# Attention's mask as a TensorE product under the scores, maxima and exponentials read from PSUM

## The chip, the cores and the metric

One core of a Trainium2 chip runs one layer of a decoder trunk. The metric is device time in microseconds of one execution, the median of several runs. Engines: TensorE (PE; PEld is its weight load), VectorE (DVE), ScalarE (ACT), GpSimd (POOL) and SyncE (SP), which issues most DMAs.

## The reference

1024 tokens of width 1024, one layer, float32. Cut to what matters here:

```python
h = x @ w_in                                  # -> q (8 heads x 64), k, v (2 x 64), conv_a, conv_gate
scores = einsum('bnqkgd,bnskd->bnkgqs', qb, kb) * 64 ** -0.5   # blocks of 128, keys of two blocks
scores = where(valid, scores, -1e30)          # window of 128: causal and not too old
m = maximum(max(scores, -1), sink)
e = exp(scores - m)
probs = e / (sum(e, -1) + exp(sink - m))
out = probs @ v
```

Beside attention a convolution group (gated, 31 taps, layer norm, swish) is computed from `conv_a` and `conv_gate`. Both go through `w_out`, a residual and a layer norm. Then comes PEER (product keys, the top 16 of 8 heads, experts from tables `peer_u` and `peer_v` of 16384 rows), a gated embedding and a last layer norm.

## The kernel before

**Tiling.** The 8 blocks of 128 tokens are split in group A (blocks 0 to 2) and group B (3 to 7). The string `ORDER` weaves generators, one for each stage and group: `q0`, `q1` (q, k and v), `c0`, `c1` (gate products of the convolution), `t0`, `t1` (its taps, 31 VectorE instructions for each of 4 channel blocks, line 351), `a0`, `a1` (attention), `l0`, `l1`, `w0`, `w1` (`w_out`), `n0`, `n1` (layer norm), `y` (PEER queries of group A), `h` and `u`. What is traced in that order is then laid out for every engine but GpSimd by a planner, which simulates the program with its own costs and lets an engine take what is ready, the earlier in the traced order first. Each engine then runs its list in order.

**Attention** (`s_att`). For each block, q and k are turned by TensorE (lines 373, 377) and copied by ScalarE (374, 379). Then `scores(g)` runs for each of two groups of four heads; one such call is called a pass below, 16 in all. It takes two PSUM banks of the pool tag `pt` (two buffers in all). The four heads lie two to a bank: heads 0 and 2 in the first, 1 and 3 in the second. The products (line 390) write `nb` x 128 columns a head: 256, or 128 in block 0, which has no block before it. Line 394 (VectorE, once a bank) scales by 0.125, adds the mask and writes `sc`, a page of SBUF. Line 400 takes the maxima, lines 401 to 403 combine them with the sink and negate, line 406 (ScalarE) makes the exponentials and their sums, 408 and 409 the reciprocals, 411 scales. `values(g)` follows up to two passes later: it turns `sc` through `pt` (line 422), copies it (423) and multiplies by v (426).

**What else uses `pt`:** the transposes of the layer norm (line 261) and those of the `u` blocks (654). The tags `ph` (four banks) and `pv` (two) hold the other products.

**Weights** (`w_split`, line 264): a DMA on SP, then ScalarE's rounded half (156) and VectorE's rest (152). The products of three halves are lines 160 to 162.

**PEER queries** (`s_query`): for each of 8 heads two products, then the scores against `keysT`, loaded by SP (line 545) into one of three buffers, and read at line 556.

Of the kernel before, what the change touches and what calls it, by code (L numbers as in the profile page):

```python
# [8 lines left out]
F32 = mybir.dt.float32  # L9
F32R = mybir.dt.float32r  # L10
BF = mybir.dt.bfloat16
I32 = mybir.dt.int32
U32 = mybir.dt.uint32
AF = mybir.ActivationFunctionType
OP = mybir.AluOpType
AX = mybir.AxisListType
# [3 lines left out]
P = 128  # L20
# [78 lines left out]
def layer(tc, io):  # L99
    nc = tc.nc  # L100
# [12 lines left out]
    def pool(name, side):  # L113
        p = tc.tile_pool(name=name, bufs=1, side=side, reuse_waits="tile")
        opened.append(p)
        return p, p.__enter__()
# [17 lines left out]
    def pt():  # L134
        return PP.tile([P, 512], F32, name="pt")
# [11 lines left out]
    def pv():  # L147
        return PP.tile([P, 512], F32, name="pv")
# [15 lines left out]
    ident = C.tile([P, P], F32, name="ident")  # L164
# [20 lines left out]
    def page(shape, dt, name):  # L185
        return PG.tile(shape, dt, name=name, tag="page", bufs=PAGES)
# [7 lines left out]
    def bcast(src, name, pool_=None):  # L194
# [4 lines left out]
    W, W_ = pool("front", "right")  # L199
# [7 lines left out]
    mask = W_.tile([P, 2 * P], BF, name="mask")  # L207
# [2 lines left out]
                            pattern=[[1, P]], channel_multiplier=-1)  # L210
    nc.gpsimd.affine_select(out=mask[:, P:], in_=mask[:, P:], compare_op=OP.is_ge, fill=-1e30, base=0,
                            pattern=[[-1, P]], channel_multiplier=1)
    ones = W_.tile([P, P], F32, name="ones")
    nc.gpsimd.memset(ones, 1.0 / 512.0)
    halo = W_.tile([P, 4, HALO], F32, name="halo")
    nc.gpsimd.memset(halo, 0.0)
    kT, vt = {}, {}
# [137 lines left out]
    def s_att(gi):  # L355

        later = []
        for j, i in enumerate(groups[gi]):
            qkv = work[i]
            rv = qkv[:, :768].rearrange("p (h d) -> p h d", d=64)  # L360
            cos = trig[:, 0, i, None, :].to_broadcast([P, 12, 8])
            sin = trig[:, 1, i, None, :].to_broadcast([P, 12, 8])
            tm = W_.tile([P, 4, 12, 8], F32, name="rot")
            nc.gpsimd.tensor_tensor(tm[:, 0], rv[:, :, 0:8], cos, op=OP.mult)
            nc.gpsimd.tensor_tensor(tm[:, 1], rv[:, :, 8:16], sin, op=OP.mult)
            nc.gpsimd.tensor_tensor(tm[:, 2], rv[:, :, 8:16], cos, op=OP.mult)
            nc.gpsimd.tensor_tensor(tm[:, 3], rv[:, :, 0:8], sin, op=OP.mult)
            nc.gpsimd.tensor_tensor(rv[:, :, 0:8], tm[:, 0], tm[:, 1], op=OP.subtract)
            nc.gpsimd.tensor_tensor(rv[:, :, 8:16], tm[:, 2], tm[:, 3], op=OP.add)
            qT = W_.tile([P, 4, P], F32, name="qT")  # L370
            ps = pt()
            for k in range(4):
                nc.tensor.transpose(ps[:, k * P:(k + 1) * P], qkv[:, k * P:(k + 1) * P], ident)
            nc.scalar.copy(qT, ps.rearrange("p (k t) -> p k t", k=4))
            ps = pt()
            for k in range(2):
                nc.tensor.transpose(ps[:, k * P:(k + 1) * P], qkv[:, 512 + k * P:512 + (k + 1) * P], ident)
            kT[i] = W_.tile([P, 2, P], F32, name="kT", bufs=3)
            nc.scalar.copy(kT[i], ps[:, :2 * P].rearrange("p (g t) -> p g t", g=2))
            nb = 2 if i else 1  # L380
            S = nb * P
            outs = {}

            def scores(g):
                sc = page([P, 4, 2 * P], F32, "sc")
                pse = [pt(), pt()]
                for pr in range(2):
                    for e in range(2):
                        for b in range(nb):
                            nc.tensor.matmul(pse[e][:, pr * S + b * P:pr * S + (b + 1) * P],  # L390
                                             qT[e * 64:e * 64 + 64, 2 * g + pr, :],
                                             kT[i + 1 - nb + b][e * 64:e * 64 + 64, g, :], start=True, stop=True)
                for e in range(2):
                    nc.vector.scalar_tensor_tensor(
                        sc[:, e::2, :S], pse[e][:, :2 * S].rearrange("p (r s) -> p r s", r=2), 0.125,
                        mask[:, None, 2 * P - S:].to_broadcast([P, 2, S]), op0=OP.mult, op1=OP.add)
                st = W_.tile([P, 3, 4], F32, name="st", bufs=4)
                nm, den, sk = st[:, 0], st[:, 1], st[:, 2]
                sg = sink[:, 4 * g:4 * g + 4]
                nc.vector.tensor_reduce(nm, sc[:, :, :S], axis=AX.X, op=OP.max)  # L400
                nc.vector.tensor_tensor(nm, nm, sg, op=OP.max)
                nc.vector.tensor_tensor(sk, sg, nm, op=OP.subtract)
                nc.vector.tensor_scalar(nm, nm, -1.0, None, op0=OP.mult)
                nc.scalar.activation(sk, sk, AF.Exp)
                for h in range(4):
                    nc.scalar.activation(sc[:, h, :S], sc[:, h, :S], AF.Exp, bias=nm[:, h:h + 1],
                                         accum_out=den[:, h:h + 1])
                nc.vector.tensor_tensor(den, den, sk, op=OP.add)
                nc.vector.reciprocal(den, den)
                for h in range(4):  # L410
                    nc.scalar.mul(sc[:, h, :S], sc[:, h, :S], den[:, h:h + 1])
                return sc

            def values(g, sc, i=i, j=j, nb=nb, outs=outs):
                if g == 0:
                    outs[0] = pv().rearrange("p (k t) -> p k t", k=4)
                po = outs[0]
                pT = page([P, 2, 2, 2, P], F32, "pT")
                for b in range(nb):
                    ps = pt()  # L420
                    for h in range(4):
                        nc.tensor.transpose(ps[:, h * P:(h + 1) * P], sc[:, h, b * P:(b + 1) * P], ident)
                    nc.scalar.copy(pT[:, b], ps.rearrange("p (k e t) -> p e k t", e=2, t=P))
                for e in range(2):
                    for b in range(nb):
                        nc.tensor.matmul(po[e * 64:e * 64 + 64, 2 * g:2 * g + 2, :],
                                         vt[i + 1 - nb + b][:, g * 64:g * 64 + 64], pT[:, b, e],
                                         start=b == 0, stop=b == nb - 1)
                if g:
                    nc.scalar.copy(work[i][:, :512].rearrange("p (k t) -> p k t", k=4), po)  # L430

            for g in range(2):
                later.append((values, g, scores(g)))
                if len(later) > LAG:
                    f, *a = later.pop(0)
                    f(*a)
                yield
        while later:
            f, *a = later.pop(0)
            f(*a)  # L440
            yield
# [94 lines left out]
    def s_query(gi):  # L536

        g = groups[gi]
        n = len(g) * P
        top = W_.tile([P, 2, len(g), 8, 2, 16], U32, name="top", tag=f"cv{gi}")  # L540
        for j, i in enumerate(g):
            tv[i], ti[i] = top[:, 0, j].bitcast(F32), top[:, 1, j]
        for h in range(8):
            keysT = W_.tile([P, 2, P], F32, name="keysT", bufs=3)
            nc.sync.dma_start(keysT, io["peer_keys_l"][h])
            qs = []
            for s in range(2):
                qT = W_.tile([P, n], F32, name="sg", bufs=3)
                by_channel(gi, w_q, 2 * h + s, lambda ps, t0, tn: nc.scalar.copy(qT[:, t0:t0 + tn], ps))  # L549
                qs.append(qT)  # L550
                if s == 0:
                    yield
            for j, i in enumerate(g):
                ps = pv()
                for s in range(2):
                    nc.tensor.matmul(ps[:, s * P:(s + 1) * P], qs[s][:, j * P:(j + 1) * P], keysT[:, s, :],
                                     start=True, stop=True)
                S = W_.tile([P, 2, P], F32, name="S", bufs=2)
                nc.scalar.copy(S, ps[:, :256].rearrange("p (s n) -> p s n", s=2))
                top16([(S[:, s, :], tv[i][:, h, s, :], ti[i][:, h, s, :]) for s in range(2)], P)  # L560
            yield
# [264 lines left out]
    for v in streams:  # L826
        if v not in "ur":
            assert next(streams[v], 0) == 0, v
    weave((s_query(1), 16), (early, UQ), (rows, RQ))
    weave((s_choose(1), 8 * nB), (early, UC), (rows, RC))  # L830
    close(W)
# [113 lines left out]
    wg, rT, r, bs = {}, {}, {}, {}  # L945
# [119 lines left out]
```

## Time and profile before

| | us |
|---|---|
| median of 3 runs (2867.88 to 2873.76) | 2872.15 |
| the profiled execution | 2867.68 |
| its span | 2865.9 |
| PE busy | 2701.1 (94%) |
| DVE busy | 2428.3 (85%) |
| ACT busy | 1151.9 (40%) |
| POOL busy | 1102.3 (38%) |

The span is the time between the first and last instruction that the profile records; the execution has 1.8 us around it. Busy shares are averages over the whole program; matmuls are pipelined, their ends modelled, so a PE that reads as fully busy need not be at its peak. [...]

### The profile page before, as it was taken

Reading aid. Unit: us, or ns where it says so; the run is one execution under the profiler, and the core shown is the slowest. Engines: PE = TensorE matmul, PEld = TensorE weight load, DVE = VectorE, ACT = ScalarE, POOL = GpSimd, SP = SyncE. Lnnn points to the kernel's source line nnn. Section 1 sums busy time; section 2 is a strip of 40 time slices with the busy share of each in tenths; the row PEclk is TensorE's granted clock in tenths of the full one; section 3 lists DMA queues with packets and bytes.
Section 4 is the critical chain, followed back from the end, with each engine's and each line's share of the span. In section 5 each row is a group of like instructions: output and inputs, shape, how many; then the busy total and the mean of one; then the engine's idle time right before and its main releaser. Section 6 shows DMA issues by size and latency. Waiting matters only on the chain. (4 is left out here: it accounts for less than half of the span.)

```text
span 2865.9 us, 45129 instructions
## 1 busy us (share of the span) xinstructions
PE 2701.1 (94%) x16785; PEld 2423.9 (85%) x16785; DVE 2428.3 (85%) x5100; ACT 1151.9 (40%) x2307; POOL 1102.3 (38%) x851
## 2 busy tenths in 40 slices
PE   7996899999989999999999999999999999999388
PEld 7974689999989999999999997887777777777288
DVE  8999769979999769888888768888887978889975
ACT  4455644533324456667666522222222222222043
POOL 0103010266680035444434445444544545454720
PEclk9997899999999999999999999999999999999689
DMA  4211233599994369999898999999999999999931
GB/s 168 74 52 41 99 124 110 183 372 325 358 318 144 126 217 378 341 366 330 328 347 325 355 352 351 337 343 341 352 335 354 340 337 343 363 349 333 336 108 46
DMA packets 266268, 774.01 MB, mean 270 GB/s; under 512 B 26688, under 2 KB 83520, under 8 KB 262976
## 3 DMA queue, kind: packets, MB, share of 16 engines
q0 software_dynamic: 110592, 402.70, 38.5%
q1 hardware_dynamic: 155456, 368.44, 35.6%
q8 instruction: 131, 2.15, 0.3%
q14 instruction: 89, 0.73, 0.1%
HBM read 681.78 MB, written 89.26 MB: 269 GB/s over the span
## 5 line engine op out<-in xcount | busy, mean ns | idle before, releaser
L767 POOL DMA_INDIRECT row<-in_peer_u_dram,ids x384 | 520.9, 1357 | 810.2 <-DVE ag L783 330.7
L767 POOL DMA_INDIRECT row<-in_peer_v_dram,ids x384 | 514.3, 1339 | 482.8 <-DVE row L775 324.9
L160 PE MATMUL ph<-acth,uu 128*128 128x320 f32 x2048 | 644.9, 315 | 0.5 <-ACT sg L549 0.3
L161 PE MATMUL ph<-actl,uu 128*128 128x320 f32 x2048 | 636.8, 311 | 0.0
L162 PE MATMUL ph<-acth,uu 128*128 128x320 f32 x2048 | 635.2, 311 | 0.0
L783 DVE SCALAR_TENSOR_TENSOR ag<-row,hb,ag 128x1024 f32<-128x1024 f32 x384 | 493.1, 1284 | 11.5 <-DMA row<-in_peer_v_dram,ids 10.6
L775 DVE SCALAR_TENSOR_TENSOR row<-row,x 128x1024 f32<-128x1024 f32 x384 | 469.3, 1225 | 12.2 <-DMA row<-in_peer_u_dram,ids 12.0
L160 PEld LDWEIGHTS ph<-acth,uu 128*128 128x128 f32 x2048 | 385.8, 188 | 3.8 <-ACT sg L549 0.9
L161 PEld LDWEIGHTS ph<-actl,uu 128*128 128x128 f32 x2048 | 385.8, 188 | 0.7
L162 PEld LDWEIGHTS ph<-acth,uu 128*128 128x128 f32 x2048 | 385.0, 188 | 0.3
L161 PE MATMUL sum<-vl,ah 128*128 128x512 f32 x896 | 353.6, 399 | 0.0
L160 PE MATMUL sum<-vh,ah 128*128 128x512 f32 x896 | 341.4, 400 | 2.4 <-ACT ah L156 2.4
L156 ACT CAST ah<-ge 128x640 fp32r<-128x640 f32 x128 | 93.1, 728 | 516.4 <-DVE ge L862 290.0
L162 PE MATMUL sum<-vh,al 128*128 128x512 f32 x896 | 266.2, 397 | 0.0
L742 ACT ACTIVATE o<-oo,rest 128x128 bf16<-128x128 bf16 x640 | 197.2, 391 | 55.5 <-DVE oo L737 55.0
L160 PEld LDWEIGHTS sum<-vh,ah 128*128 128x128 f32 x896 | 170.6, 190 | 45.9 <-ACT ah L156 4.6
L161 PEld LDWEIGHTS sum<-vl,ah 128*128 128x128 f32 x896 | 170.7, 191 | 41.4
L693 ACT ACTIVATE ge<-ph 128x320 f32<-128x320 f32 x256 | 107.7, 436 | 239.4 <-PE ph L162 170.8
L162 PEld LDWEIGHTS sum<-vh,al 128*128 128x128 f32 x896 | 168.9, 189 | 41.3 <-DVE al L152 0.4
L152 DVE TENSOR_TENSOR vl<-raw,vh 128x1024 fp32r<-128x1024 f32 x128 | 155.1, 1221 | 54.2 <-ACT vh L156 54.1
L160 PE MATMUL part<-vh,ah 128*128 128x512 f32 x384 | 157.5, 410 | 42.9 <-DVE acc L910 22.1
L156 ACT CAST vh<-raw 128x1024 fp32r<-128x1024 f32 x128 | 129.3, 1045 | 153.4 <-PE part L162 102.7
(297 smaller groups left out, 5388.5 us busy)
## 6 DMA issues: line engine op xcount, KB each, us to landing
raw<-in_peer_v_dram SPq DMA_DIRECT2D x128, 512.0 KB, 7.4
raw<-in_peer_u_l_dram SPq DMA_DIRECT2D x82, 512.0 KB, 7.3
g_dr<-stage SPq DMA_DIRECT2D x20, 2048.0 KB, 10.5
gt<-g_dr SPq DMA_DIRECT2D x21, 1920.0 KB, 16.8
e_dr<-ge SPq DMA_DIRECT2D x122, 320.0 KB, 5.8
ge<-e_dr SPq DMA_DIRECT2D x122, 320.0 KB, 7.2
uraw<-in_peer_u_dram SPq DMA_DIRECT2D x45, 512.0 KB, 4.1
wraw<-in_peer_query_l_dram SPq DMA_DIRECT2D x32, 512.0 KB, 5.5
```

Source lines behind the costliest of these rows:

```text
L152: return eng.tensor_tensor(o, a, b, op=OP.subtract)
L156: nc.scalar.copy(hi, src)
L160: nc.tensor.matmul(ps, lh, rh, start=first, stop=False)
L161: nc.tensor.matmul(ps, lh, rl, start=False, stop=False)
L162: nc.tensor.matmul(ps, ll, rh, start=False, stop=last)
L693: nc.scalar.activation(ge[:, c0:c0 + cn], o, AF.Gelu)
L742: nc.scalar.mul(o2[:, 2, e], oo[:, 1, e], rest[:, t + e:t + e + 1])
L767: nc.gpsimd.indirect_dma_start(out=t, out_offset=None, in_=table, in_offset=bass.IndirectOffsetOnAxis(ap=ids[i][:, s:s + 1], axis=0))
L775: behind(nc.vector.scalar_tensor_tensor(u, u, 1.0, x1, op0=OP.mult, op1=OP.mult, accum_out=hb[:, e:e + 1]), marks, TIE)
L783: behind(nc.vector.scalar_tensor_tensor(ag, v, blocks[b][:, e:e + 1], ag, op0=OP.mult, op1=OP.add), marks, TIE)
```

## The change

The mask goes into PSUM first: TensorE multiplies an identity in bf16 (`one`) by the mask, broadcast to the two heads of a bank, and the scores accumulate on it. The pre-scaled copy `sc` by VectorE is gone. The maxima read PSUM, one instruction for each bank; the factor 0.125 moves into the instruction that combines them with the sink and into ScalarE's exponentials, which read PSUM and write `sc`. `one` is a new tile in the pool that also holds `keysT`, whose buffers go from three to two.

```diff
+    one = W_.tile([P, P], BF, name="one")
+    nc.vector.tensor_copy(one, ident)
...
             def scores(g):
                 sc = page([P, 4, 2 * P], F32, "sc")
                 pse = [pt(), pt()]
+                both = [t[:, :2 * S].rearrange("p (r s) -> p r s", r=2) for t in pse]
+                for e in range(2):
+                    nc.tensor.matmul(both[e], one, mask[:, None, 2 * P - S:].to_broadcast([P, 2, S]),
+                                     start=True, stop=False, skip_group_check=True)
                 for pr in range(2):
                     for e in range(2):
                         for b in range(nb):
                             nc.tensor.matmul(pse[e][:, pr * S + b * P:pr * S + (b + 1) * P],
                                              qT[e * 64:e * 64 + 64, 2 * g + pr, :],
-                                             kT[i + 1 - nb + b][e * 64:e * 64 + 64, g, :], start=True, stop=True)
-                for e in range(2):
-                    nc.vector.scalar_tensor_tensor(
-                        sc[:, e::2, :S], pse[e][:, :2 * S].rearrange("p (r s) -> p r s", r=2), 0.125,
-                        mask[:, None, 2 * P - S:].to_broadcast([P, 2, S]), op0=OP.mult, op1=OP.add)
+                                             kT[i + 1 - nb + b][e * 64:e * 64 + 64, g, :], start=False,
+                                             stop=pr == 1 and b == nb - 1, skip_group_check=True)
...
-                nc.vector.tensor_reduce(nm, sc[:, :, :S], axis=AX.X, op=OP.max)
-                nc.vector.tensor_tensor(nm, nm, sg, op=OP.max)
+                for e in range(2):
+                    nc.vector.tensor_reduce(nm[:, e::2], both[e], axis=AX.X, op=OP.max)
+                nc.vector.scalar_tensor_tensor(nm, nm, 0.125, sg, op0=OP.mult, op1=OP.max)
...
                 for h in range(4):
-                    nc.scalar.activation(sc[:, h, :S], sc[:, h, :S], AF.Exp, bias=nm[:, h:h + 1],
-                                         accum_out=den[:, h:h + 1])
+                    nc.scalar.activation(sc[:, h, :S], both[h % 2][:, h // 2, :], AF.Exp, bias=nm[:, h:h + 1],
+                                         scale=0.125, accum_out=den[:, h:h + 1])
...
-            keysT = W_.tile([P, 2, P], F32, name="keysT", bufs=3)
+            keysT = W_.tile([P, 2, P], F32, name="keysT", bufs=2)
```

## Rows read from the trace of the kernel before

**Rows 1.** The page's 40 slices of the span, busy share in tenths.

```profile
PE   7996899999989999999999999999999999999388
...
DVE  8999769979999769888888768888887978889975
```

**Rows 2.** Stages: length, then busy us (instructions) of each engine, granted clock, DMA.

```profile
107.00:200.00 93.00, 93.00 (x595) 80.97 (x593) 86.38 (x147) 50.83 (x124) 3.37 (x6) 1.00 0.18 58
200.00:305.00 105.00, 78.92 (x373) 54.15 (x372) 100.43 (x152) 53.50 (x130) 23.89 (x28) 0.82 0.17 56
305.00:353.00 48.00, 39.80 (x202) 26.39 (x199) 31.82 (x66) 34.60 (x88) 0.00 (x0) 0.79 0.28 99
353.00:450.00 97.00, 95.94 (x477) 84.56 (x477) 65.35 (x204) 37.90 (x61) 7.20 (x8) 1.00 0.39 123
```

**Rows 3.** Instructions on the tile sc: ns min/median/max, first and last start, forms.

```profile
L406 ACT ACTIVATE sc<-sc,st x64: 387/495/523, 120.3 to 340.5; 128x256 f32<-128x256 f32 x56, 128x128 f32<-128x128 f32 x8
...
L394 DVE SCALAR_TENSOR_TENSOR sc<-pt,mask x32: 407/684/694, 107.1 to 336.5; 128x512 f32<-128x512 f32 x28, 128x256 f32<-128x256 f32 x4
L400 DVE TENSOR_REDUCE st<-sc x16: 671/1215/1223, 109.9 to 337.2; 128x4 f32<-128x1024 f32 x14, 128x4 f32<-128x512 f32 x2
```

**Rows 4.** The taps, from the instructions on the tile cv.

```profile
L351 DVE SCALAR_TENSOR_TENSOR cv<-hc,cw,cv x240: 586/800/1706, 31.6 to 302.0; 128x384 f32<-128x384 f32 x61, 128x640 f32<-128x640 f32 x59
```

**Rows 5.** TensorE in order of time: start, us, instruction; two pairs of 512-column products.

```profile
205.14 0.40 PE L160 MATMUL ph<-wh,actah 128*128 128x512 f32 x1
205.37 0.39 PE L161 MATMUL ph<-wl,actah 128*128 128x512 f32 x1
...
235.66 0.63 PE L161 MATMUL ph<-wl,actah 128*128 128x512 f32 x1
236.09 0.63 PE L160 MATMUL ph<-wh,actah 128*128 128x512 f32 x1
```

**Rows 6.** VectorE in order of time, from 255 to 336 us.

```profile
255.01 1.27 DVE L394 SCALAR_TENSOR_TENSOR sc<-pt,mask 128x512 f32<-128x512 f32 x2
...
265.26 0.16 DVE L403 TENSOR_SCALAR st<-st 128x4 f32<-128x4 f32 x1
...
312.75 0.69 DVE L394 SCALAR_TENSOR_TENSOR sc<-pt,mask 128x512 f32<-128x512 f32 x1 [1.19 <-PE pt L390]
...
335.43 0.69 DVE L394 SCALAR_TENSOR_TENSOR sc<-pt,mask 128x512 f32<-128x512 f32 x1 [1.57 <-PE pt L390]
```

**Rows 7.** ScalarE in order of time, from 256 to 318 us.

```profile
256.44 1.18 ACT L423 COPY pT<-pt 128x512 f32<-128x512 f32 x2 [0.39 <-PE pt L422]
...
268.49 0.19 ACT L406 ACTIVATION_READ_ACCUMULATOR sc<-sc,st 128x1 f32 x1
...
317.81 0.19 ACT L406 ACTIVATION_READ_ACCUMULATOR sc<-sc,st 128x1 f32 x1
```

**Rows 8.** TensorE in order of time, 216 to 354 us, idle before and releaser in brackets.

```profile
216.08 1.26 PE L390 MATMUL pt<-kT,qT 64*128 64x128 f32 x16
...
231.20 0.80 PE L160 MATMUL ph<-wh,actah 128*128 128x512 f32 x1 [9.21 <-ACT wh L156]
...
255.75 1.25 PE L422 MATMUL pt<-ident,sc 128*128 128x128 f32 x8 [1.02 <-DVE sc L394]
...
274.40 1.97 PE L422 MATMUL pt<-ident,sc 128*128 128x128 f32 x8 [6.47 <-ACT sc L411]
...
330.36 1.94 PE L261 MATMUL pt<-ident,work 128*128 128x128 f32 x8 [3.02 <-DVE work L506]
...
353.33 0.79 PE L160 MATMUL ph<-actah,wh 128*128 128x384 f32 x3 [0.24 <-ACT actah L156]
```

**Rows 9.** SP's own waits (total us, times, longest), and the landing of keysT's loads.

```profile
SPq L545 <- PE pv L556: 59.8, 12, 13.4
...
DMA to landing us min/median/max: 1.9/3.9/10.3
```

**Rows 10.** A copy of 256 elements from PSUM, from the instructions on the tile S.

```profile
L559 ACT COPY S<-pv x64: 359/373/405, 366.5 to 884.2; 128x256 f32<-128x256 f32 x64
```

## The prediction

> **What bounds the kernel now.** I read the page's slices first, then a table of stages, then the instructions that the change touches, then the order of time on three engines. The slices [rows 1] show TensorE at 9 nearly everywhere except in slices 3 to 5 (about 215 to 355 us), at the start and at the end. The only part where time can be won or lost by attention is therefore the stretch up to 353 us, where the first matmul of the PEER queries starts [rows 8]; from there TensorE is busy for 95.94 of 97 us [rows 2], and an earlier or later start there moves the rest of the program by the same amount. Attention itself runs from 107 to 353 us, in three stages [rows 2]:
> - 107 to 200 us: TensorE 93.00 of 93 busy, VectorE 86.38 of 93. TensorE is the bound, VectorE close behind.
> - 200 to 305 us: VectorE 100.43 of 105, TensorE 78.92 at a granted clock of 0.82. VectorE is the bound; it works off the convolution taps, the last of which starts at 302.0 us [rows 4], with attention's and the weights' pieces among them. TensorE stands still behind it: 9.21 us for a weight cast that waited for VectorE's half of an earlier split, 6.47 us for normalised scores whose reciprocals VectorE made late [rows 8].
> - 305 to 353 us: VectorE 31.82 of 48, TensorE 39.80. No engine is full. A chain goes on: last `w_out` products, layer norm, its transposes (TensorE waits 3.02 us for line 506), the query product [rows 8].
>
> Attention is 16 passes (8 blocks, 2 groups of heads); 6 fall in the first stage, 7 in the second, 3 in the third. Two of the first six are the half-wide ones of block 0.
>
> **What VectorE loses and gains.** A full pass has two line-394 instructions of 0.684 us and one line-400 maximum over 1024 elements of 1.215 us [rows 3]: 2.58 us. After the change it has two maxima over 512 elements. No row shows a maximum read from PSUM; from below stands the half-wide line 400 (512 elements from SBUF, 0.671), from above line 394 (512 from PSUM with a second operand, 0.694) [rows 3]. I take 0.68, between ends that nearly meet: 1.36 us, so 1.22 saved. A pass of block 0 goes from 2 x 0.407 + 0.671 = 1.485 to about 2 x 0.40: 0.69 saved. Over 14 and 2 passes: 18.4 us. The scaled maximum in place of the plain one is one small instruction for another, and the copy that makes `one` runs once in the first microseconds: nothing for both, because each is one instruction of 4 or 128 elements.
>
> [...]
>
> **What becomes of it by stage.** 200 to 305: VectorE is the bound, 7 passes x 1.22 = 8.5 us, taken whole. 107 to 200: 4 x 1.22 + 2 x 0.69 = 6.3 us of VectorE beside a full TensorE. It is worth something only where VectorE uses it to take taps out of the second stage; it already stands idle there for 6.6 us, so I take half, 3 us (bounds 0 and 6.3). 305 to 353: 3 x 1.22 = 3.7 us, on the chain only where the layer norm's instructions queue behind a pass; I take 1 (0 to 3.7). Together 12.5 us.
>
> **What TensorE gains.** 32 mask products: 28 of 512 columns, 4 of 256. No 512-column product in bf16 is in these rows; fp32r ones of that width follow each other at 205.14 and 205.37, a step of 0.23 us at full clock, and at 235.66 and 236.09, 0.43 us, at half [rows 5]. Nothing in the rows makes bf16 slower; bounds 0.12 (half a step) and 0.43 us; I take 0.23. In the first stage, where TensorE is the bound, that is 8 x 0.23 + 4 x 0.12 = 2.3 us on the path. In the second its 14 x 0.23 = 3.2 us lie in 26 us of idle time; in the third 6 x 0.23, of which nothing is certain to count. So 2.3 us (1.4 to 6.0 with the clock and the third stage).
>
> **What ScalarE gains.** The 64 exponentials, 0.495 us from SBUF [rows 3], now read PSUM and scale by 0.125. Line 559 copies 256 elements from PSUM in 0.373 [rows 10]. So 64 times between 0 and -0.12 us; ScalarE is half busy in these stages [rows 2], I take 0.
>
> **The banks.** The two `pt` banks come free when line 394 has read them; afterwards they are held until the fourth exponential has. Behind that wait stand, in `pt`'s order, the transposes of earlier scores, those of the next q and k, and the next pass's scores. Among the taps: line 394 starts at 255.01, line 403 comes at 265.26, the last accumulator is read at 268.49 [rows 6, 7], so the banks would be held for 13.7 - 1.2 = 12.5 us. After the taps: 312.75 to 317.81 and 0.19, 5.25, less 1.2 = 4.0 us. The other work on `pt` in a pass is about 4.5 us (estimate: scores 1.26, two transposed halves from 255.75 to the end of the copies at 257.62 [rows 7, 8], and some 1.3 for half of a block's q and k). The passes follow each other now every (335.43 - 255.01) / 7 = 11.5 us [rows 6]. Held time and work come to 17.0 us among the taps, which is more than 11.5, and to 8.5 after them, which is less. A pass that comes late among the taps leaves VectorE free for the taps, so they end sooner, and the late passes catch up at 3 us each. What VectorE needs is not changed by the order, so in the second stage I set no price on the hold beyond what half of stage one and most of stage three have already lost. Bounds: 0, and 4 passes x 5.5 = 22 us late.
>
> [...]
>
> The scores' page is first written by the exponentials instead of by line 394, so it may be held for less; I count nothing (0 to a few tenths at each transfer that waits for a page).
>
> **keysT with two buffers.** SP waits 59.8 us in all at these loads, 12 times; a load lands in 3.9 us [rows 9]. With one buffer less a load waits for the scores of the head two before its own, not three before; the `w_q` and `peer_u` loads queue behind it on SP. It still has a whole head's products as cover. I take 0; if that cover were gone, up to 13 loads x 3.9 = 51 us.
>
> **Sum.** -12.5 + 2.3 = -10 us on the profiled execution's own 2867.7 (its span 2865.9 and 1.8 around it): 2857.7. That run lies 4.5 us under the median of the three runs, 2872.15, so for a median I add these: 2862.
>
> **Rivals.**
> 1. The bank hold decides (slower). Place: blocks 4 and 5, while taps still run. It decides when the hold exceeds 11.5 - 4.5 = 7 us in four passes and TensorE has no other ready product. Price: 22 late, less 3 x 3.0 = 9 caught up in the third stage, plus 2.3 for the masks: +15, so 2887. For it: 12.5 us by the rows. Against: VectorE is the true bound there, and the hold shrinks as taps run out.
> 2. The two cancel: the hold eats what VectorE saves, or the saved time finds no taps ready. -10 to the hold's +10: 2866 to 2878, within 0.2%. For it: TensorE is full in the first stage and the third has no full engine.
> 3. All of VectorE's 18.4 us arrives: 2854. For it: VectorE's 100.43 of 105. Against: stages one and three.
> 4. The keys' loads, or the order in which the planner lays the work anew, cost more than they bring: two or three key loads uncovered, 3 x 3.9 = +12, 2884 (slower). Against: no row shows TensorE waiting for keys.
>
> **How the numbers follow.** A measurement of this kernel can tell about 0.2%, 5.7 us, from no change. Forecast (-6 to -15) 0.38, rival 3 0.10: faster 0.48. Rival 2: same 0.24. Rival 1 0.18, rival 4 0.10: slower 0.28. The range runs from a little below rival 3 to just short of rival 1's price, 2848 to 2884; the likeliest case's own is 2857 to 2866.
>
> **What would show it.** Right: no scaled copy on VectorE, 32 maxima of about 0.68 us from `pt`; the last tap before 295 us; the first query product (line 160 on 128x384) at about 343 instead of 353.3; TensorE's idle time in 200 to 350 smaller. Wrong: TensorE waiting for `pt` behind the exponentials, with VectorE well under 95% busy before 300 us; taps ended early and that first query product no earlier; or a start gained at 345 and lost by 500 us at the keys.

## The result: 35 us slower, and the profile after

The changed kernel takes 2908.25 us (median of 4 runs, 2902.79 to 2914.52) beside 2872.95 us (2867.88 to 2873.81) for the kernel before: ratio 1.0124, 95% interval 1.0103 to 1.0146. The forecast was 2862 us, range 2848 to 2884. The profiled execution took 2914.52 us (span 2912.7). In the changed kernel's lines the mask products are L391, the scores L396, the maxima L404, their small followers L405 to L408, the exponentials L410, the reciprocals L413, the scaling L415, the transposes of scores L426, the copies behind them L427, the values L430 and the taps L353.

The page's slices, to be laid beside [rows 1]:

```profile
PE   7987789999989999999999999999999999999488
...
DVE  8987356998999949988888858888879888889975
```

VectorE's fourth and fifth slices (218 to 364 us) fell from 9 and 7 to 7 and 3, but TensorE's third to sixth read 8778 where they read 9689: the freed engine did not fill the other. The stages (length, busy us and instructions of PE, PEld, DVE, ACT and POOL, granted clock as a share of full speed, DMA share, GB/s), the first three against [rows 2]; the last line is the whole stretch up to the first query product:

```profile
107.00:200.00 93.00, 84.86 (x504) 73.68 (x502) 87.35 (x144) 40.11 (x94) 4.31 (x6) 0.91 0.17 53
200.00:305.00 105.00, 76.31 (x339) 51.98 (x338) 73.78 (x114) 51.62 (x123) 16.41 (x28) 0.77 0.13 44
305.00:353.00 48.00, 40.33 (x179) 27.36 (x179) 16.35 (x33) 21.07 (x56) 0.00 (x0) 0.73 0.19 60
353.00:400.00 47.00, 30.69 (x133) 19.02 (x130) 21.09 (x47) 24.07 (x62) 0.00 (x0) 0.67 0.20 73
...
107.00:407.70 300.70, 239.82 (x1190) 176.65 (x1188) 202.43 (x344) 141.75 (x343) 20.72 (x34) 0.80 0.16 53
```

The same stretch of the kernel before, up to its own first query product:

```profile
107.00:353.30 246.30, 211.82 (x1165) 161.51 (x1163) 218.63 (x363) 139.24 (x342) 27.26 (x34) 0.88 0.19 65
```

VectorE is relieved as planned (218.63 to 202.43 us) and is far from full in every stage but the first. TensorE has 60.9 us without work (300.70 - 239.82) where it had 34.5 (246.30 - 211.82), and its busy time is 28.0 us longer at a mean granted clock of 0.80 instead of 0.88. Together these are the 54.4 us by which the first query product is late.

The instructions themselves (ns min/median/max, first and last start, forms), from the tiles st, mask, cv and sc:

```profile
L404 DVE TENSOR_REDUCE st<-pt x32: 413/684/692, 106.0 to 386.3; 128x2 f32<-128x512 f32 x28, 128x2 f32<-128x256 f32 x4
...
L391 PE MATMUL pt<-mask,one x32: 282/389/650, 104.1 to 383.7; 128*128 128x512 bf16 x28, 128*128 128x256 bf16 x4
...
L353 DVE SCALAR_TENSOR_TENSOR cv<-hc,cw,cv x240: 585/799/1707, 30.6 to 271.6; 128x384 f32<-128x384 f32 x61, 128x640 f32<-128x640 f32 x59
...
L410 ACT ACTIVATE sc<-pt,st x64: 349/473/492, 115.2 to 389.1; 128x256 f32<-128x256 f32 x56, 128x128 f32<-128x128 f32 x8
L426 PE MATMUL pt<-ident,sc x120: 270/417/477, 154.5 to 401.5; 128*128 128x128 f32 x120
```

The last tap starts 30.4 us earlier than in [rows 4], and the last exponential 48.6 us later than in [rows 3]: the two streams came apart. Half of the transposes L426 now run at 0.417 us and above; the shortest take 0.270. The waits between 107 and 420 us (us in total, times, longest):

```profile
ACT st L408 <- DVE st L406: 49.9, 11, 10.7
PEld pt L426 <- ACT sc L410: 39.8, 9, 8.6
PE pt L426 <- ACT sc L410: 37.4, 9, 8.4
DVE st L404 <- PE pt L396: 27.4, 13, 4.8
```

TensorE waits for the exponentials, VectorE for TensorE's scores, and ScalarE for VectorE's maxima: a ring. In the kernel before the largest wait of TensorE at `pt` was the single 6.47 us of [rows 8]. One turn of the ring after the taps: first TensorE in order of time (start, us, instruction, idle time before it and what ended it), then VectorE's maxima and ScalarE's exponentials in the same stretch:

```profile
312.16 1.97 PE L426 MATMUL pt<-ident,sc 128*128 128x128 f32 x8 [3.32 <-ACT sc L410]
314.05 1.12 PE L430 MATMUL pv<-pT,acc 128*64 128x256 f32 x2
315.10 0.61 PE L391 MATMUL pt<-mask,one 128*128 128x512 bf16 x1
315.64 2.07 PE L396 MATMUL pt<-kT,qT 64*128 64x128 f32 x8
317.64 1.97 PE L430 MATMUL pv<-pT,acc 128*64 128x256 f32 x6
319.55 0.61 PE L391 MATMUL pt<-mask,one 128*128 128x512 bf16 x1
320.09 2.07 PE L396 MATMUL pt<-kT,qT 64*128 64x128 f32 x8
325.11 1.97 PE L426 MATMUL pt<-ident,sc 128*128 128x128 f32 x8 [2.95 <-ACT sc L410]
```

```profile
317.75 0.69 DVE L404 TENSOR_REDUCE st<-pt 128x2 f32<-128x512 f32 x1 [4.79 <-PE pt L396]
...
322.20 0.69 DVE L404 TENSOR_REDUCE st<-pt 128x2 f32<-128x512 f32 x1 [3.76 <-PE pt L396]
...
323.58 0.47 ACT L410 ACTIVATE sc<-pt,st 128x256 f32<-128x256 f32 x1
...
324.49 0.47 ACT L410 ACTIVATE sc<-pt,st 128x256 f32<-128x256 f32 x1
...
324.94 0.48 ACT L410 ACTIVATE sc<-pt,st 128x256 f32<-128x256 f32 x1
```

The first bank's maxima start at 317.75, but no exponential can start before the second bank's, at 322.20, are reduced and combined. So the first bank is held from 315.10 until its second exponential (the third of the four, at 324.49) ends at 324.96, and the transposes of the scores of the pass before (325.11) can only start then. Nothing else of TensorE's stands in between: from 322.16 to 325.11 it has no work. The first query product, against the last line of [rows 8]:

```profile
407.76 0.79 PE L160 MATMUL ph<-actah,wh 128*128 128x384 f32 x3
```

### The profile page after: what moved, and what is told of

The parts are those of the page before. It is cut to its first block, busy times and chain, and to the rows that moved or that the text cites. A ratio compares the mean times of both kernels' runs of the same rounds, so it can differ in the third digit from the quotient of the medians.

```text
span 2912.7 us, 45192 instructions
## 1 busy us (share of the span) xinstructions
PE 2729.4 (94%) x16817; PEld 2439.8 (84%) x16817; DVE 2413.0 (83%) x5085; ACT 1154.2 (40%) x2309; POOL 1077.1 (37%) x851
## 3 DMA queue, kind: packets, MB, share of 16 engines
q1 hardware_dynamic: 155456, 368.44, 35.1%
## 5 line engine op out<-in xcount | busy, mean ns | idle before, releaser
L771 POOL DMA_INDIRECT row<-in_peer_v_dram,ids x384 | 495.4, 1290 | 484.2 <-DVE row L779 325.8
L779 DVE SCALAR_TENSOR_TENSOR row<-row,x 128x1024 f32<-128x1024 f32 x384 | 466.9, 1218 | 12.5 <-DMA row<-in_peer_u_dram,ids 12.3
L162 PE MATMUL sum<-vh,al 128*128 128x512 f32 x896 | 275.5, 397 | 0.4 <-DVE al L152 0.4
L746 ACT ACTIVATE o<-oo,rest 128x128 bf16<-128x128 bf16 x640 | 197.2, 391 | 55.0 <-DVE oo L741 54.4
L152 DVE TENSOR_TENSOR vl<-raw,vh 128x1024 fp32r<-128x1024 f32 x128 | 154.7, 1219 | 43.8 <-ACT vh L156 43.6
```

The lines of the kernel that those rows point to most:

```text
L152: return eng.tensor_tensor(o, a, b, op=OP.subtract)
L162: nc.tensor.matmul(ps, ll, rh, start=False, stop=last)
L746: nc.scalar.mul(o2[:, 2, e], oo[:, 1, e], rest[:, t + e:t + e + 1])
L771: nc.gpsimd.indirect_dma_start(out=t, out_offset=None, in_=table, in_offset=bass.IndirectOffsetOnAxis(ap=ids[i][:, s:s + 1], axis=0))
L779: behind(nc.vector.scalar_tensor_tensor(u, u, 1.0, x1, op0=OP.mult, op1=OP.mult, accum_out=hb[:, e:e + 1]), marks, TIE)
```

## Experiments

Theory A: the loss is the time for which the two `pt` banks are held until the exponentials. Rivals: B, the mask products on TensorE; C, the buffer that keysT lost, or the new layout; D, VectorE or ScalarE themselves. Twelve further kernels were run, and three kernels were profiled a second time. The planner lays the program anew for every edit, and no run forces the old order on it, so each run shows an edit together with the order that it brings. Each ratio is to the kernel before on the same chip, with its 95% interval. "Idle" is the length of the stretch from 107 us to the first query product less TensorE's busy time in it, and "clock" the granted clock there, from the profile of each run:

| kernel | ratio | last tap | first query product | idle | clock |
|---|---|---|---|---|---|
| before | 1 | 302.0 | 353.3 | 34.5 | 0.88 |
| after | 1.0124 (1.0103 to 1.0146) | 271.6 | 407.8 | 60.9 | 0.80 |
| keys2 | 1.0003 (0.9990 to 1.0017) | 304.0 | 355.9 | 35.1 | 0.86 |
| mask_only | 1.0004 (0.9986 to 1.0022) | 297.2 | 354.7 | 31.8 | 0.91 |
| hold_only | 1.0240 (1.0218 to 1.0261) | 273.0 | 425.0 | 89.5 | 0.77 |
| act_copy | 0.9975 (0.9964 to 0.9985) | 280.6 | 362.2 | 31.6 | 0.89 |
| no_max_wait | 0.9984 (0.9968 to 1.0000) | 281.6 | 362.6 | 30.6 | 0.86 |
| exp_order | 1.0091 (1.0073 to 1.0110) | 267.8 | 391.1 | 52.8 | 0.84 |
| half_pass | 1.0087 (1.0066 to 1.0108) | 273.5 | 379.1 | 46.8 | 0.87 |
| one_copy | 1.0116 (1.0096 to 1.0137) | 277.7 | 390.9 | 44.1 | 0.83 |
| pt3_after | 1.0208 (1.0190 to 1.0227) | 299.8 | 390.8 | 43.8 | 0.87 |
| pt3_before | 0.9984 (0.9969 to 0.9998) | 305.6 | 347.6 | 22.6 | 0.92 |
| act_copy_pt3 | 1.0021 (1.0010 to 1.0032) | 297.8 | 354.4 | 22.4 | 0.92 |
| relief_only | 0.9978 (0.9966 to 0.9991) | 281.7 | 348.1 | 31.9 | 0.88 |

Second profiles of before, after and act_copy (at the end of this section) put the first query product at 358.1, 398.9 and 361.1, so single values of that column are good to some 9 us.

**keys2**: the kernel before with the two small edits of the change.

```diff
+    one = W_.tile([P, P], BF, name="one")
+    nc.vector.tensor_copy(one, ident)
-            keysT = W_.tile([P, 2, P], F32, name="keysT", bufs=3)
+            keysT = W_.tile([P, 2, P], F32, name="keysT", bufs=2)
```

> The kernel before with two keysT buffers and the unused tile one added; nothing of attention changed. Hold theory (two pt banks kept from the scores to the exponentials make the passes of attention follow each other one by one): no change, 2873 within 6 us, first query product at about 353 us. Rival (keysT or the shifted layout is what costs): 2890 or more.

2874.94 us beside 2874.77, and the first query product at 355.9. C falls.

**mask_only**: the change, but VectorE copies the banks as before, and maxima and exponentials read the copy.

```diff
+                for e in range(2):
+                    nc.vector.tensor_scalar(sc[:, e::2, :S], both[e], 0.125, None, op0=OP.mult)
-                    nc.vector.tensor_reduce(nm[:, e::2], both[e], axis=AX.X, op=OP.max)
+                nc.vector.tensor_reduce(nm, sc[:, :, :S], axis=AX.X, op=OP.max)
```

> The change with TensorE's mask products, but VectorE scales both banks into SBUF as before (0.125, no mask) and maxima and exponentials read that copy: the banks come free as early as before, TensorE has all 32 extra products. Hold theory: within 6 us of before, 2870 to 2880. Rival (the mask products on TensorE, or their half-clock steps, cost the time): most of the loss stays, 2895 or more.

2874.25 us beside 2874.77. B falls: the 32 mask products cost nothing that can be measured (the interval leaves room for 6 us of the 35).

**hold_only**: the kernel before, with its VectorE work, where ScalarE reads one element of each bank behind the four exponentials. That adds 32 instructions of 0.242 us on ScalarE, and the banks come free only behind them. `keysT` has two buffers here too, which by keys2 costs nothing.

```diff
+                for e in range(2):
+                    junk = W_.tile([P, 1], F32, name="junk", bufs=2)
+                    nc.scalar.activation(junk, pse[e][:, :1], AF.Copy, scale=den[:, 2 + e:3 + e])
```

> The kernel before (mask and scaled copy by VectorE), with two keysT buffers and one addition: after the four exponentials of a pass ScalarE reads one element a partition of each of the two score banks, so the banks stay taken as long as in the changed kernel. 32 small ScalarE instructions of about 0.2 us more. Hold theory: slower than before by 30 us or more, attention's last pass after 370 us, because VectorE also keeps its 18 us. Rival (mask products or keysT): within 10 us of before.

2944.22 us beside 2874.77, 69 us slower. Its waits between 107 and 420 us, and its first query product:

```profile
PEld pt L425 <- ACT junk L410: 62.2, 9, 13.7
ACT st L404 <- DVE st L402: 60.2, 11, 9.0
PE pt L425 <- ACT junk L410: 59.9, 9, 13.5
DVE sc L394 <- PE pt L390: 30.2, 12, 5.4
```

```profile
424.99 0.79 PE L160 MATMUL ph<-actah,wh 128*128 128x384 f32 x3
```

The ring of the changed kernel is there, line by line, with no mask product and no maximum read from PSUM. A alone makes the kernel slower, and by more than the change does; here VectorE keeps its copies and the two reads lengthen the hold, and how the extra divides between these was not tried.

**act_copy**: the change, with ScalarE copying and scaling each bank as soon as its scores stand; the maxima read PSUM, the exponentials the copy.

```diff
+                for e in range(2):
+                    nc.scalar.activation(sc[:, e::2, :S], both[e], AF.Copy, scale=0.125)
-                    nc.scalar.activation(sc[:, h, :S], both[h % 2][:, h // 2, :], AF.Exp, bias=nm[:, h:h + 1],
-                                         scale=0.125, accum_out=den[:, h:h + 1])
+                    nc.scalar.activation(sc[:, h, :S], sc[:, h, :S], AF.Exp, bias=nm[:, h:h + 1],
+                                         accum_out=den[:, h:h + 1])
```

> The change with one more step: ScalarE copies each bank, scaled, to SBUF as soon as the scores are there (32 copies, about 0.58 us for 512 columns), and the exponentials read that copy; maxima still from PSUM by VectorE. The banks come free after a maximum and a copy and not after the exponentials. Hold theory: most of the 35 us comes back, 2860 to 2885. Rival (mask products, keysT): 2900 or more.

2869.63 us beside 2874.77: the loss is gone, and this kernel beats both. The copies, from its tile sc:

```profile
L401 ACT ACTIVATE sc<-pt x32: 375/592/601, 106.2 to 344.8; 128x512 f32<-128x512 f32 x28, 128x256 f32<-128x256 f32 x4
```

Some 18 us more work on ScalarE (28 x 0.592 + 4 x 0.375) buy the way from 1.0124 to 0.9975: the banks are given back early, and that is the difference between the two kernels. D falls too: VectorE reads its maxima from PSUM as in the change, ScalarE has more to do, and nothing is lost.

**no_max_wait**: the change with a bias of zero in the exponentials, which then don't wait for the maxima. It leaves out the subtraction of the maximum.

```diff
-                    nc.scalar.activation(sc[:, h, :S], both[h % 2][:, h // 2, :], AF.Exp, bias=nm[:, h:h + 1],
+                    nc.scalar.activation(sc[:, h, :S], both[h % 2][:, h // 2, :], AF.Exp, bias=zero,
```

> The change, but the exponentials take a bias of zero and so don't wait for the maxima, which are still made (left out: the subtraction of the maximum in the exponentials). The banks are held for the maxima or the exponentials, whichever is later, without the way over VectorE's queue between them. Hold theory: the hold falls by the 0.8 us of the three small instructions after the taps and by 5 us or more among them; 2880 to 2898. Rival (the length of the hold among the taps is covered anyway): 2900 to 2912.

2865.56 us beside 2870.99, below the 2880 to 2898 of theory A: the expectation left the four exponentials' own time as a loss, and there was none. What costs is not that ScalarE reads the banks, but that it reads them behind the maxima. This run shortens the hold and also takes VectorE out of the way from the scores to the exponentials; act_copy, where the exponentials still wait for the maxima, is the one that tells the two apart.

**exp_order**: the change with the exponentials of bank 0 (heads 0 and 2) first.

```diff
-                for h in range(4):
+                for h in (0, 2, 1, 3):
```

> The change with the exponentials in the order of heads 0, 2, 1, 3, so the first bank comes free after two of them and not after three. Hold theory: 0.45 us a pass for one of the two banks, at most 16 x 0.45 = 7 us: 2900 to 2908. Rival: nothing, 2908.

2897.71 us beside 2870.99, a little under the expected 2900 to 2908: about a quarter of the loss returns, from giving one bank back an exponential (0.47 us) earlier in each pass. The 0.0033 between the two ratios are some 9 us, beside 7.5 us for the exponential's own time over 16 passes. That is as if the delay of a pass were handed on in full, but the intervals of the two ratios touch (1.0103 and 1.0110), so it is not shown.

**half_pass**: maxima, small instructions and exponentials for one bank at a time.

```diff
+                for e in range(2):
+                    nme, ske = nm[:, e::2], sk[:, e::2]
+                    nc.vector.tensor_reduce(nme, both[e], axis=AX.X, op=OP.max)
...
+                    for h in (e, e + 2):
+                        nc.scalar.activation(sc[:, h, :S], both[e][:, h // 2, :], AF.Exp, bias=nm[:, h:h + 1],
```

> The change, with the maximum, the negation and the exponentials done for one bank (two heads) at a time, so that the first bank is given back before the second one's maxima are known; 3 more small VectorE instructions a pass (about 0.5 us). If the loss is the time for which both banks are held together: better than the other order of the exponentials (1.0091), 2880 to 2897. If a late VectorE decides more than the two banks: no better than the change, 2905 to 2915.

2894.39 us beside 2872.59. Inside the band of theory A, but its ratio can't be told from that of exp_order. The query products start 12 us earlier than there (379.1), little more than two profiles of one kernel differ by; the end does not show it.

**one_copy**: ScalarE copies only bank 1 early; bank 0 is held until its two exponentials, which come first.

```diff
+                nc.scalar.activation(sc[:, 1::2, :S], both[1], AF.Copy, scale=0.125)
-                for h in range(4):
+                for h in (0, 2, 1, 3):
```

> The change, with one of the two banks copied and scaled by ScalarE early (0.6 us a pass), its exponentials taken from the copy; the other bank is still held until its two exponentials, which come first. If the loss goes with the time that banks are held: between the other order (1.0091) and the copy of both banks (0.9975), near 2880. If one held bank is as bad as two, since the next pass needs both: 2890 to 2905.

2904.12 us beside 2872.59, at the upper end of the second case: one held bank is about as bad as two. That this is so because each pass needs both is the expectation's reason and not shown; the interval overlaps that of the change, and that of exp_order too.

**pt3_after** and **pt3_before**: three `pt` banks and three `ph` banks instead of two and four, in the change and in the kernel before.

```diff
-        return PP.tile([P, 512], F32, name="pt")
+        return PP.tile([P, 512], F32, name="pt", bufs=3)
-        return PP.tile([P, 512], F32, name="ph", bufs=4)
+        return PP.tile([P, 512], F32, name="ph", bufs=3)
...
-        pss = [(ph() if j < 4 else pv())[:, :cn] for j in range(len(g))]
+        pss = [(ph() if j < 3 else pv())[:, :cn] for j in range(len(g))]
```

> The change with a third pt bank, taken from ph (four to three; the fifth block of group B then uses pv). Scores still hold two banks until the exponentials, but transposes have one of their own. Hold theory: TensorE's waits for the exponentials at the transposes go, and the time falls by 10 us or more against the same change of banks in the kernel before plus the 35 us of the change; 2875 to 2900 if the smaller ph costs nothing. Rival (what counts is the serial chain of a pass, not who else needs the banks): no better than the changed kernel, 2900 or more.

> The kernel before with three pt and three ph banks: what the exchange of banks costs or brings by itself. Both theories: 2865 to 2890; it is the one to set beside the other kernel with three pt banks.

pt3_before took 2867.41 us beside 2870.99. pt3_after was a miss for theory A: 2931.33 us, slower than the change, in the range of the rival (the serial chain of a pass is what counts). In attention the third bank does part of what A says: TensorE's idle time falls from 60.9 to 43.8 us, and the query products start 17 us earlier (8 against the second profile of the change). But they then take longer to the first instruction of the gates: 689.8 us instead of 671.4 (390.8 to 1080.6, and 407.8 to 1079.2). In pt3_before this stretch is 688.0 instead of 674.9 (347.6 to 1035.6, and 353.3 to 1028.2). So the exchange of banks costs 13 to 18 us there. The traces show where: TensorE's waits for ScalarE's copies of the key scores, at `pv`, are 21.9 us instead of 9.9, and 20.5 instead of 11.4. Whether the missing fourth `ph` bank does it, or the order that the planner then lays, was not separated. It accounts for pt3_after being no better than the change at the gates; behind them it loses another 6 us in the dense stage (937 us from first to last product, 931 in the change) and 5 after it, which is not explained.

**act_copy_pt3**: both together, a try for more.

> The change with ScalarE's early copy of both banks, and three banks for scores against three for the products behind them. Each of the two alone was a little faster than before (0.9975 and 0.9984). If the two gains are of different waits: 2855 to 2862, faster than both kernels. If the third bank gains only what the lost fourth bank of the later stages gives back: 2862 to 2872.

2877.43 us beside 2872.59: outside both cases. Query products at 354.4, gates at 1047.4, 693.0 us between them instead of act_copy's 672.7: the exchange of banks again.

**relief_only**: the kernel before, its maximum over 8 of 256 columns (it leaves out the rest of the maximum).

```diff
-                nc.vector.tensor_reduce(nm, sc[:, :, :S], axis=AX.X, op=OP.max)
+                nc.vector.tensor_reduce(nm, sc[:, :, S - P:S - P + 8], axis=AX.X, op=OP.max)
```

> The kernel before, except that the maximum of a pass is taken over 8 of the 256 columns: it leaves out the rest of the maximum, and so 16 of the reductions of 1.215 us shrink to some 0.16 (about 17 us of VectorE), while the score banks are given back as before. If VectorE's load is what sets attention's length, as the prediction's 8.5 + 3 + 1 us assumed: first query product 10 us or more earlier than 353.3, kernel 2855 to 2863. If attention's passes are held by their own chain through the two banks and VectorE's time is worth little there (in the runs without the hold, attention ended no earlier than before): first query product within 5 us of 353.3, last tap of the convolution some 15 us earlier, kernel 2866 to 2872.

2867.51 us beside 2872.59. The reduction, from its tile sc:

```profile
L400 DVE TENSOR_REDUCE st<-sc x16: 130/176/187, 108.6 to 331.4; 128x4 f32<-128x32 f32 x16
```

That is 14 x 1.215 + 2 x 0.671 - 16 x 0.176 = 15.5 us less on VectorE, with [rows 3] for the first two, and no bank held longer. The taps end 20 us earlier, the query products start 5.2 us earlier, and the kernel gains 5 to 6 us (3 to 10 by the interval), inside the second case: about a third of what VectorE was spared.

**before_again**, **after_again**, **act_copy_again**: a second profile of three kernels, one run each.

> The kernel before, profiled a second time, to see how much of its dense stage (939 us from its first product to its last in the first profile) belongs to the kernel and how much to the one execution. If to the kernel: 937 to 941 us again. If to the execution: a different length, by several us. The start of the query products in attention (353.3) should come within 3 us in either case.

> The change, profiled a second time. Its dense stage was 931 us, 8 us under that of before, which is how a start of the query products 54 us late became an end 47 us late. If the shorter stage belongs to the kernel: 929 to 933 us again. If to the execution: it comes out elsewhere between 925 and 943.

> The version with ScalarE's early copy of both banks, profiled a second time: its query products started 9 us later than before's, and it is 5 us faster at the end. If its dense stage (929 us) belongs to the kernel: 927 to 931 us again, and the gain over before is made there. If to the execution: it comes out elsewhere, and the gain of 0.25% is not explained by that stage.

They took 2877.41, 2901.77 and 2863.90 us, with query products at 358.1, 398.9 and 361.1; the first is 4.8 us late where 3 were expected at most. The dense stage's products on the tile sum (ns, first and last start), first and second profile of each; before:

```profile
L160 PE MATMUL sum<-vh,ah x896: 391/397/629, 1726.2 to 2665.3; 128*128 128x512 f32 x180
```

```profile
L160 PE MATMUL sum<-vh,ah x896: 391/397/632, 1728.1 to 2675.4; 128*128 128x512 f32 x180
```

After:

```profile
L160 PE MATMUL sum<-vh,ah x896: 391/397/628, 1777.2 to 2707.9; 128*128 128x512 f32 x180
```

```profile
L160 PE MATMUL sum<-vh,ah x896: 391/397/628, 1769.7 to 2695.2; 128*128 128x512 f32 x180
```

act_copy:

```profile
L160 PE MATMUL sum<-vh,ah x896: 391/397/628, 1732.9 to 2662.2; 128*128 128x512 f32 x180
```

```profile
L160 PE MATMUL sum<-vh,ah x896: 392/397/628, 1729.9 to 2652.9; 128*128 128x512 f32 x180
```

From first to last this is 939 and 947 us before, 931 and 926 after, 929 and 923 in act_copy. It spreads by 5 to 8 us between executions, so no kernel kept to its first value; but the pairs don't overlap, and the change's stage is 15 us shorter on average. From that first product on TensorE has the same 4,864 instructions in both, in another order: the planner laid the work behind attention anew. The length goes with such an order rather than with the change: keys2, which has the order of the kernel before there, takes 942 us, and pt3_before, without the change and in an order of its own, takes 927. What in the order does it is open.

## Why the prediction was wrong

**The step that failed: "in the second stage I set no price on the hold".** The prediction measured the hold from the last copy's end to the fourth exponential, 4.0 us after the taps, added 4.5 us of other work on `pt`, and found 8.5 under the 11.5 us between passes, so that "the late passes catch up at 3 us each". In the changed kernel the first maxima of passes follow each other every 14.5 us after the taps ((383.78 - 282.47) / 7, from VectorE in order of time):

```profile
282.47 1.29 DVE L404 TENSOR_REDUCE st<-pt 128x2 f32<-128x512 f32 x2 [1.59 <-PE pt L396]
...
383.78 0.69 DVE L404 TENSOR_REDUCE st<-pt 128x2 f32<-128x512 f32 x1 [2.08 <-PE pt L396]
```

The term of that sum that was mis-sized most is the 4.5 us of other work. In the turn shown with the result, the time from one pass's transposes to the next one's is 12.95 us (312.16 to 325.11): 10.0 us of TensorE's own work and 2.95 us of waiting for the exponentials. Three things make the 10.0. First, the products L430, which hold no `pt` bank, stand between the others in TensorE's order of time (from 314.05 and from 317.64, 3.1 us in all), so they are in the ring too. Second, in the second pass of a block the banks are filled one behind the other, and each bank's 8 score products by themselves take nearly as long as 16 of both banks together: 1.16 us at a granted clock of 1.00, against 1.26 in [rows 8], at 1.00 too. Third, at the granted clock of 0.50 of the turn shown they take 2.07:

```profile
210.76 1.16 PE L396 MATMUL pt<-kT,qT 64*128 64x128 f32 x8
```

The hold itself was too small where the banks are filled one behind the other: bank 0 then stands 4.45 us (317.75 to 322.20) waiting only for bank 1's scores, and from the first maximum to the start of the last of four exponentials (324.94) it is 7.2 us. In the pass before, whose banks were filled together, it is 3.3 us (308.65 to 311.99), near the prediction's 4.0. That 4.0 was also read from the wrong row: 312.75 in [rows 6] is the copy of the second bank alone, and the first bank's was earlier:

```profile
310.88 0.68 DVE L394 SCALAR_TENSOR_TENSOR sc<-pt,mask 128x512 f32<-128x512 f32 x1
```

So the same pass gave a hold of 6.4 us for bank 0 (311.56 to 318.00) and 4.6 for bank 1, not 4.0 for both.

The late passes did not catch up; six instead of three are left after 305 us. hold_only shows that the hold alone does this, act_copy and no_max_wait that without it nothing is lost.

How much of the 28.0 us of longer busy time the clock makes was not tried by itself (the mean granted clock is 0.73 instead of 0.79 between 305 and 353 us, and 0.65 instead of 0.77 between 260 and 305). An estimate from the traces, which takes TensorE's speed to go with its clock (the 8 score products' 1.16 us at 1.00 and 2.07 at 0.50 are near that): busy time weighted with the granted clock, slice by slice of 1 us, comes to 192.4 us before and 196.9 in the change, so some 4 or 5 of the 28 us are more work and the rest a lower clock. The second profiles of the two kernels, each up to its own first query product, show that this part is not steady:

```profile
107.00:358.11 251.11, 217.35 (x1159) 164.52 (x1157) 217.84 (x361) 139.18 (x342) 27.33 (x34) 0.86 0.19 63
107.00:398.94 291.94, 229.15 (x1185) 169.26 (x1184) 202.13 (x343) 141.50 (x344) 20.61 (x34) 0.82 0.16 55
```

There the busy time is only 11.8 us longer. What both pairs share is TensorE's idle time, 26 and 29 us more. The masks are about the 4 us of more work (mask_only's busy time grew by 4.1), and not the cause of the idle time, which fell there.

Point by point:

- **VectorE's durations: right.** 0.684 us for a maximum of 512 elements from PSUM (taken: 0.68), 0.413 for the half-wide one. Against the half-wide maximum of 512 elements from SBUF in [rows 3], 0.671, the one from PSUM takes 13 ns more.
- **"Together 12.5 us": too much by half.** relief_only has 15.5 of the 18.4 us and none of the hold; it gained 5 to 6. "VectorE is the bound" from 200 to 305 us was read from its 100.43 busy us. But what was freed brought the taps forward (302.0 to 281.7) more than attention (353.3 to 348.1).
- **Masks +2.3: within the measurement of nothing** (mask_only 0.9986 to 1.0022). **keysT 0: right** (keys2). **ScalarE 0: right within its bounds**; an exponential takes 0.473 us from PSUM and 0.495 from SBUF, 1.4 us less over all 64.
- **"An earlier or later start there moves the rest of the program by the same amount": off by some 12 us.** The query products start 54 and 41 us late in two pairs of profiles, 48 on average; the spans grow by 47 and 24, 36 on average, near the medians' 35. The difference is made in the dense stage, which is 15 us shorter, less 4 us that come back behind it. This also places act_copy's gain: its query products start 9 and 3 us late, and its median ends 5 us early.
- **Rival 1 named the mechanism and the sign; its chance (0.18) and its price (+15) were too low.** It looked for the loss "while taps still run" and let the third stage give 9 us back. The loss is on both sides: 8 us of TensorE's work are already missing by 200 us (84.86 instead of 93.00), and after the taps it grows instead of shrinking. What it needed was one sum: a pass with its steps laid end to end, TensorE's whole list and both banks included, at the clock of that stage. For the turn shown that is the 12.95 us above, more than the 11.5 between passes; the price of 35 us does not follow from it alone.
- **"What would show it"** named the signs that came: TensorE waiting for `pt` behind the exponentials, VectorE at 73.78 of 105 us, and taps that end early with a first query product that doesn't.

## What to carry to other kernels

When an edit moves the reading of a PSUM bank to a later consumer, price the bank first: lay one pass end to end from a bank's first product to its last reader, with every bank that a reader waits for and all that stands between in the engines' lists, and compare that with the period between passes (12.95 us in the turn shown, against 11.5). A copy that looks superfluous may be what gives the bank back; if it must go from one engine, put it on another with time to spare (here ScalarE, whose 18 us of copies took the ratio from 1.0124 to 0.9975), rather than leave it out. And test a "bound" read from busy time by taking the load away: 15 us less on VectorE, over 95% busy from 200 to 305 us, gave 5 to 6.

## What was not expected of the hardware

A bank taken from one stage was paid for in another: with a third `pt` bank TensorE's idle time in attention fell by 12 us in pt3_before (34.5 to 22.6), and with three `ph` banks instead of four the query products behind it took 13 to 20 us longer, in all three pairs; the part of the planner's order in this was not separated. A bank's score products alone cost nearly what both banks' cost together (8 in 1.16 us, 16 in 1.26, both at a clock of 1.00), and in the turn shown, where the banks are filled one behind the other, it is 7.2 us from the first maximum to the start of the last exponential, in the pass before 3.3. And where TensorE waited longer its granted clock was lower: with 34.5, 60.9 and 89.5 us idle (before, after, hold_only) the mean in the stretch was 0.88, 0.80 and 0.77, and the same 8 products take 1.16 us at 1.00 and 2.07 at 0.50. That the waits bring the clock down was not tried by itself, and the order isn't strict (no_max_wait has 30.6 us idle at 0.86).
